# A gMLP and dilated-attention layer on one core: values re-laid in DRAM, projection weights in longer rows, and a warm-up bank of its own

## The chip, the core and the metric

The kernel runs on one core of a Trainium2 chip. The core has a matrix engine (TensorE, PE in the profile, with its weight loads shown apart as PEld), a vector engine (VectorE, DVE), a scalar engine (ScalarE, ACT), a general engine (GpSimd, POOL) and a sync engine (SyncE, SP) that here only issues DMA transfers. Each engine works through its own list of instructions in order; semaphores make an instruction wait for one on another engine or for a transfer. The metric is the device time of one execution in microseconds. It is the median of several executions, and the profile is that of one of them.

## The reference

One layer, sequence 1024, model width 1024, all in float32. Cut to what matters:

```python
h = rms_norm(x, g_pre)
u_a, v_a, z_a, q_b, k_b, v_b, z_b, gate_a, gate_b = split(h @ w_in)   # widths 3 x 2048, then 6 x 1024
y_a = spatial_gating(gelu(u_a), gelu(v_a), ln_g, ln_b, w_s, b_s) * silu(z_a)
# spatial_gating: u * (W_s LayerNorm(v) + b), W_s mixing 128 positions for each of 16 channel groups
y_b = mixture_of_dilations(q_b, k_b, v_b) * silu(z_b)
# 8 heads of 128; windows (128, dilation 1), (512, 4), (2048, 16), each +-64 keys, ALiBi,
# the three outputs weighted by their softmax denominators
m = sigmoid(gate_a + b) * (y_a @ w_pa) + sigmoid(gate_b + b) * (y_b @ w_pb)
out = x + rms_norm(m @ w_o, g_post)
```

## The kernel before

Every float32 operand of a matmul is split into a high and a low part (`hi`, `lo`), and a product is three matmuls: hi·hi, hi·lo, lo·hi. For a weight, `operand()` (L104 to L109) does the split: ACT copies the raw tile to `wh_...` (L106), then POOL, or DVE in a few places, subtracts to get `wl_...` (L108). Raw weight tiles `wr_...` come from DRAM through `raw_tile()` (L111 to L114), always on the SP queue, into three buffers, or into two buffers of another pool for the second half of a block.

The program has these stages.

1. **Start** (to about 60 us). Eight tiles of x are loaded, normalised (`norm_tile`, L244) and transposed on PE into the matrices `hT00`, `hT01`, `hT10`, `hT11`, together with sums of quarters of h (`t1` to `t4`). Warm-up matmuls on a tile of zeros (`warm`, L227) run ahead, around the product that spreads the gain vector over 128 partitions (`gpre`, L231 to L235). The bank with the tag "tp" that the warm-up writes is also the bank that the squares of `norm_tile` (`sqx`, L253) write.
2. **Values of the attention** (`vb`, to about 150 us), eight products of 128 rows each in two column halves. Their split halves go to DRAM, `v_hi` and `v_lo`, 1024 rows of 1024 each.
3. **Values of the gMLP** (`va0` to `va3`, about 161 to 322 us). Each group is one Strassen-like block of seven products, `p1, p6, p2, p7, p5, p4, p3` (`STEPS`, L377). A product of a group is 48 matmuls. Product `p1` needs the first half of the raw weights alone (tiles `wr_va100` and `wr_va101` for group 1: group, half j, quarter q), product `p6` needs `s2 = w10 + w11 - w00`, which DVE computes (L391) from the first half and the second half (`wr_va110`, `wr_va111`). The results pass gelu on ACT (`v_use`, L523), DVE takes statistics (L525), and SP stores them to `v_d` (L527), eight stores a group.
4. **Loop over g = 0, 2, ..., 14** (about 322 to 1020 us). Each iteration computes `u` and `z` for two channel groups, then one to two further blocks (`q`, `k`, `zb` for two heads, or gates), and between their products the spatial mixing of the normalised `vn`, read back from `v_d`. The blocks are the same seven products of 12 matmuls each (`features`, L443). Block u0 reads `wr_u00` for `p1` and `wr_u00` with `wr_u01` for `p6`.
5. **Attention** (about 1020 to 1330 us), eight heads, with the product of the gMLP branch, `y_a @ w_pa`, put between their pieces (`mlp_products`, L911 to L916). Its weights come from `mlp_weights` (L883), 32 loads of 512 KB, each a tile of eight 128-row blocks by 128 columns, held for two operands. The attention values of a head come by `residue_values` (L636) and `chunk_values` (L644): the chunk values lie row by row of one residue modulo 4, so that a head takes 4 residues x 2 halves x 2 pieces (`va`, the inner seven chunks, and `ve`, both ends) = 16 transfers.
6. **Tail** (to the end): the product with `w_pb`, the gates, `w_o`, the closing norm.

The Python text issues work in the order above, but the order in which an engine meets its instructions is set by the framework's list scheduler: it takes ready instructions by its own costs and priorities, so that a load stands in the SP queue where the scheduler put it, not where the text has it. `tc.issue_after(x)` tells it to put an instruction behind x. A store on the SP queue waits there until its data are computed, and what stands behind it on that queue waits with it.

## Time and profile before

| | |
|---|---|
| time, median of three runs | 1565.2 us (1562.21 to 1565.73) |
| the profiled execution's own time | 1563.55 us |
| its span in the profile | 1561.8 us, 22765 instructions |
| PE busy | 1511.7 us (97%) |
| PE weight loads | 1275.1 us (82%) |
| DVE, POOL, ACT busy | 872.5, 780.5, 683.0 us |
| DMA traffic | 251.64 MB, mean 161 GB/s |
| granted PE clock, mean | 0.99 |

The profile's page lists busy time of each engine, the span in 40 slices, the DMA queues, the chain of work that ended last, the costliest groups of instructions and the DMA issues with their time to landing. The trace behind it can be asked for stretches of time: what each engine did, what an instruction waited for, and the granted clock. A row of the timeline gives the start, the duration, the engine, the line of the kernel, the operation, output and inputs by name, a count, and in brackets the idle time ahead of it with the engine whose work ended it. Engine names with a q (SPq) are the issues of a DMA on that engine's queue. Tile names there are cut short: `va0u` is any tile of group va0 whose name begins so.

### The profile page before, as it was taken

To read this page: it belongs to the slowest core of one execution; us is meant where nothing else is said; L and a number is where in the kernel's file an instruction comes from. 1 tells how busy PE (TensorE), PEld (TensorE's weight loads), DVE (VectorE), ACT (ScalarE), POOL (GpSimd) and SP (SyncE) were. 2 spreads that over 40 slices of the span, in tenths; PEclk is the share of its full clock that TensorE was granted. 3 is DMA by queue.
4 is the path that set the end of the run, shared out by engine and by line. 5 is a ranking of instruction groups with operands and counts; after the bars stand their busy time and mean duration, and the time that the engine had idled before them with its cause. 6 is when DMAs were issued, how large, how long until landed. Compare 5 with 4: busy or idle time off the path is not lost.

```text
span 1561.8 us, 22765 instructions
## 1 busy us (share of the span) xinstructions
PE 1511.7 (97%) x7865; PEld 1275.1 (82%) x7865; DVE 872.5 (56%) x1699; ACT 683.0 (44%) x1318; POOL 780.5 (50%) x711
## 2 busy tenths in 40 slices
PE   8999999999999999999999999998999889999998
PEld 4787999988888888788888888877887778878886
DVE  5622544476665675766665565567877768232112
ACT  5522433343443433343445454577666755431111
POOL 2322644465565555555555555536555545473132
PEclk9999999999999999999999999999999999999999
DMA  6445533343434453544534353388687765885531
GB/s 230 162 135 190 161 109 102 113 130 123 153 121 148 126 171 115 152 138 138 165 108 156 101 176 109 123 244 255 201 226 199 225 209 179 250 270 166 187 108 68
DMA packets 247798, 251.64 MB, mean 161 GB/s; under 512 B 14297, under 2 KB 187385, under 8 KB 247426
## 3 DMA queue, kind: packets, MB, share of 16 engines
q1 hardware_dynamic: 247456, 249.88, 51.1%
q8 instruction: 62, 1.02, 0.3%
q14 instruction: 54, 0.44, 0.1%
q10 hardware_dynamic: 226, 0.30, 0.1%
HBM read 173.58 MB, written 76.55 MB: 160 GB/s over the span
## 4 chain that ended last, share of the span: by engine, by line
PE 71%; DVE 9%; issue 7%; ACT 4%; POOL 4%; DMA 4%; SPq 0%; ACTq 0%; POOLq 0%; DVEq 0%
PE pb L1040 2%; PE pb L1041 2%; PE pb L1039 2%; PE vb L154 2%; PE vb L156 2%; PE vb L155 2%; PE sg L560 2%; PE pa L916 2%; PE pa L914 2%; PE pa L915 2%; ACT st L704 1%; POOL out L1060 1%; PE pr L791 1%; DMA vn<-v_d 1%; DVE st L752 1%
## 5 line engine op out<-in xcount | busy, mean ns | idle before, releaser
L108 POOL TENSOR_TENSOR wl_pa<-wr_pa,wh_pa 128x512 fp32r<-128x512 f32 x56 | 74.6, 1342 | 42.3 <-ACT wh_pa L106 32.7
L704 ACT ACTIVATE st<-st,own 128x256 f32<-128x256 f32 (+1 forms) x128 | 62.6, 493 | 36.1 <-DVE own L700 36.1
L549 DVE TENSOR_SCALAR vn<-vn,mean,rstd 128x128 f32<-128x128 f32 x128 | 56.6, 497 | 36.4 <-DMA vn<-v_d 36.0
L1039 PE MATMUL pb<-yh,wh_pb 128*128 128x512 f32 x128 | 49.9, 390 | 2.0 <-ACT yh L159 2.0
L106 ACT ACTIVATE wh_pa<-wr_pa 128x512 fp32r<-128x512 f32 x64 | 38.7, 623 | 28.1 <-DMA wr_pa<-in_w_proj_a_dram 19.6
L1040 PE MATMUL pb<-yl,wh_pb 128*128 128x512 f32 x128 | 50.0, 391 | 0.4 <-DVE yl L159 0.2
L1041 PE MATMUL pb<-yh,wl_pb 128*128 128x512 f32 x128 | 49.8, 389 | 0.0
L717 DVE COPY oth<-own 32x4 f32<-32x4 f32 x128 | 36.2, 283 | 14.8 <-ACT st L704 13.3
L1074 ACT ACTIVATE sq<-o 128x512 f32<-128x512 f32 x16 | 9.6, 598 | 74.6 <-PE o L1072 74.6
L159 POOL TENSOR_TENSOR vl<-vn,vh 128x512 fp32r<-128x512 f32 x32 | 41.3, 1292 | 0.8 <-ACT vh L159 0.8
L1043 POOL TENSOR_TENSOR mb<-thb,mb 128x512 f32<-128x512 f32 x16 | 20.6, 1287 | 41.7 <-DVE thb L1042 28.1
L159 POOL TENSOR_TENSOR qcl<-q,qch 128x512 fp32r<-128x512 f32 x16 | 27.1, 1699 | 28.6 <-ACT qch L159 28.6
L717 POOL COPY oth<-own 32x4 f32<-32x4 f32 x128 | 24.0, 188 | 30.9 <-ACT st L704 26.2
L1054 DVE TENSOR_TENSOR sso<-sso 128x1 f32<-128x1 f32 x8 | 1.3, 160 | 67.6 <-ACT sq L1074 67.6
L752 DVE TENSOR_SCALAR st<-st,nm 128x256 f32<-128x256 f32 x64 | 38.1, 637 | 0.3
L164 POOL TENSOR_TENSOR sso<-sso,mhalf 128x1 f32<-128x1 f32 x8 | 4.4, 550 | 59.1 <-DVE sso L163 59.1
L159 DVE TENSOR_TENSOR ptlb<-pb,pthb 128x512 fp32r<-128x512 f32 x32 | 22.0, 687 | 20.5 <-ACT pthb L159 20.5
L859 POOL TENSOR_TENSOR o<-o,zt 128x512 f32<-128x512 f32 x16 | 20.6, 1291 | 25.7 <-DMA zt<-z_d 13.7
L108 POOL TENSOR_TENSOR wl_wos<-wr_wos,wh_wos 128x512 fp32r<-128x512 f32 x16 | 20.7, 1291 | 22.8 <-ACT wh_wos L106 22.8
L700 DVE CUSTOM_DVE_ANT_0 st<-sc,tb 128x256 f32<-128x256 f32 x64 | 23.5, 416 | 14.0 <-PE sc L697 12.6
L1039 PEld LDWEIGHTS pb<-yh,wh_pb 128*128 128x128 f32 x128 | 24.0, 188 | 7.4 <-ACT yh L159 2.4
L772 PE MATMUL pb<-ident,st 128*128 128x128 f32 x128 | 21.0, 286 | 8.3 <-DVE st L752 5.5
(2648 smaller groups left out, 5842.0 us busy)
## 6 DMA issues: line engine op xcount, KB each, us to landing
wr_pa<-in_w_proj_a_dram SPq DMA_DIRECT2D x32, 512.0 KB, 5.8
wr_g<-in_w_in_dram SPq DMA_DIRECT2D x16, 512.0 KB, 3.6
wr_va<-in_w_in_dram SPq DMA_DIRECT2D x16, 512.0 KB, 3.7
wr_u<-in_w_in_dram SPq DMA_DIRECT2D x16, 512.0 KB, 4.0
wr_z<-in_w_in_dram SPq DMA_DIRECT2D x16, 512.0 KB, 4.0
vn<-v_d SPq DMA_DIRECT2D x32, 256.0 KB, 3.1
y_d<-s SPq DMA_DIRECT2D x32, 256.0 KB, 2.4
wr_yf<-y_d SPq DMA_DIRECT2D x16, 512.0 KB, 5.0
```

The costliest lines, as they stand in the source:

```text
L106: nc.scalar.activation(hi, src, AF.Copy)
L108: low.tensor_tensor(lo, src, f32(hi), ALU.subtract)
L154: nc.tensor.matmul(ps, lhs[k][0], rh, start=(k == 0), stop=False)
L155: nc.tensor.matmul(ps, lhs[k][0], rl, start=False, stop=False)
L159: return nc.scalar.activation(hi, src, AF.Copy), low.tensor_tensor(lo, src, f32(hi), ALU.subtract)
L549: nc.vector.tensor_scalar(vn[:, c, :], vn[:, c, :], mean[:, 4 * b + c, 0:1], rstd[:, 4 * b + c:4 * b + c + 1], op0=ALU.subtract, op1=ALU.mult)
L704: nc.scalar.activation(st[:, t, :n], st[:, t, :n], AF.Exp, bias=own[:, half, idx, 0:1], scale=-1.0, accum_out=own[:, half, idx, 1:2])
L717: (nc.gpsimd, nc.vector)[half].tensor_copy(dst, src)
L752: nc.vector.tensor_scalar(w, w, f, None, op0=ALU.mult)
L1039: nc.tensor.matmul(ps, lh, rh, start=(k == 0), stop=False)
L1040: nc.tensor.matmul(ps, lh, rl, start=False, stop=False)
L1041: nc.tensor.matmul(ps, ll, rh, start=False, stop=(k == KT - 1))
```

## The change

Three edits.

- **The warm-up bank.** The warm-up matmuls write a bank with the tag "sc" in place of "tp", and there is one more of them ahead of the `gpre` product. The two ACT copies that take the spread gain out of its bank move behind the squares of the first tile.
- **Attention values in the chunks' row order.** New DRAM tensors `va_d` (7 x 4 x 32 rows of 1024, high and low) and `ve_d` (2 x 4 x 16 rows of 1024, high and low) hold copies of the rows of `v_hi` and `v_lo`, sorted by chunk and residue. `value_rows()` makes them with 24 transfers from DRAM to DRAM on the SP queue: 8 of 7 x 32 x 1024 floats (917 KB each) and 16 of 16 x 1024 floats (64 KB each). The text takes one of its eight steps at the head of each iteration of the g loop. `chunk_values` then reads a head's values with four transfers. The bytes that a head reads stay the same, and so does the length of a contiguous piece (128 floats).
- **Projection weights.** `mlp_weights` loads tiles of four 128-row blocks by 256 columns, so that a contiguous piece is 1 KB in place of 512 bytes. The number of loads (32) and their size (512 KB) stay. Two raw tiles now feed four operands together (before, one fed two), and the second of the four already needs the second tile; the buffers for raw tiles stay three.

```diff
@@ -176,6 +176,9 @@
         return [dram.tile(shape, F32, name=f"{name}_{s}") for s in "hl"]
 
     v_hi, v_lo = hi_lo("vb", [S, DB])
+
+    va_d = hi_lo("va", [7, 4, 32, DB])
+    ve_d = hi_lo("ve", [2, 4, 16, DB])
     o_d = dram.tile([H, P, S], F32, name="o_d")
     t4_d = hi_lo("t4", [P, 4, 512])
     q_d = dram.tile([H, P, S], F32, name="q_d")
@@ -222,16 +225,16 @@
         nc.scalar.activation(first[:, P:P + 1], mhalf, AF.Square)
         idle = wpool.tile([P, 512], BF16, tag="th", bufs=2, name="idle")
         nc.vector.memset(idle, 0.0)
-        pt = bank("tp", "warm")
+        pt = bank("sc", "warm")
 
         def warm(n):
             for _ in range(n):
                 nc.tensor.matmul(pt, idle[:, :P], idle, start=True, stop=True)
 
-        warm(4)
-        for j, pg in enumerate(banks("mm mm", "gpre")):
+        warm(5)
+        spread = banks("mm mm", "gpre")
+        for j, pg in enumerate(spread):
             nc.tensor.matmul(pg, ones, grow[:, 512 * j:512 * (j + 1)], start=True, stop=True)
-            nc.scalar.activation(gpre[:, 512 * j:512 * (j + 1)], pg, AF.Copy)
         warm(8)
 
         def transposed(hl, i, src, name):
@@ -242,7 +245,7 @@
             split(*[t[:, :, i * P:(i + 1) * P] for t in hl], pt.rearrange("p (k n) -> p k n", k=4))
             return last
 
-        def norm_tile(c, load=1):
+        def norm_tile(c, load=1, between=None):
             b, i = divmod(c, 4)
             for _ in range(load):
                 load_tile()
@@ -251,6 +254,8 @@
             sq = bank("tp", f"sqx{c}")
             for j in range(2):
                 squared = nc.scalar.activation(sq, xt[:, 512 * j:512 * (j + 1)], AF.Square, accum_out=ss[:, j:j + 1])
+            if between:
+                between(squared)
             nc.vector.tensor_tensor(ss[:, 0:1], ss[:, 0:1], ss[:, 1:2], ALU.add)
             power(ss[:, 1:2], ss[:, 0:1], 1.0 / D)
             for j in range(2):
@@ -318,7 +323,12 @@
             nc.scalar.activation(wb, pb, AF.Copy)
             nc.sync.dma_start(wsb_d[q].rearrange("p g n -> p (g n)"), wb)
 
-        squared, turned = norm_tile(0, 0)
+        def norm_weights(squared):
+            for j, pg in enumerate(spread):
+                with tc.issue_after(squared.ins):
+                    nc.scalar.activation(gpre[:, 512 * j:512 * (j + 1)], pg, AF.Copy)
+
+        squared, turned = norm_tile(0, 0, norm_weights)
         rows = sp.tile([32, P], F32, name="rows")
         wv = []
         for k in range(0, KT, 2):
@@ -579,8 +589,19 @@
             lambda h=h: features(w_in, OFF_K + h * P, f"k{h}", store_parts(k_d[h:h + 2])),
             lambda h=h: features(w_in, OFF_ZB + h * P, f"zb{h}", gate_z(h)))]
         others += [lambda m=m: gates(m) for m in range(2, 16, 2)]
+        def value_rows():
+
+            for vd, va_, ve_ in zip((v_hi, v_lo), va_d, ve_d):
+                for r in range(4):
+                    nc.sync.dma_start(va_[:, r], vd[64:960].rearrange("(a i r) n -> r a i n", i=32, r=4)[r])
+                    for c in range(2):
+                        nc.sync.dma_start(ve_[c, r], vd[960 * c:960 * c + 64].rearrange("(i r) n -> r i n", r=4)[r])
+                    yield
+
+        rows_moved = value_rows()
         for g in range(0, G, 2):
             us, ts = {}, {}
+            take(rows_moved, 1)
 
             def u_use(i, b, _, c, src):
                 nc.scalar.activation(c, src, AF.Gelu_apprx_tanh)
@@ -645,14 +666,11 @@
 
             hs = slice(h * P, (h + 1) * P)
             res["va"], res["ve"] = [], []
-            for s, vd in enumerate((v_hi, v_lo)):
+            for s in range(2):
                 a_ = ap.tile([P, 7, E], F32R, tag=f"va{s}", name=f"va{s}{h}")
                 e_ = ap.tile([64, 2, E], F32R, tag=f"ve{s}", name=f"ve{s}{h}")
-                va_src = vd[64:960, hs].rearrange("(a i r) e -> r i a e", i=32, r=4)
-                ve_src = vd.rearrange("(c i r) n -> r i c n", i=16, r=4)
-                for r in range(4):
-                    nc.sync.dma_start(f32(a_[32 * r:32 * (r + 1)]), va_src[r])
-                    nc.sync.dma_start(f32(e_[16 * r:16 * (r + 1)]), ve_src[r][:, 0:16:15, hs])
+                nc.sync.dma_start(f32(a_), va_d[s].rearrange("a r i n -> (r i) a n")[:, :, hs])
+                nc.sync.dma_start(f32(e_), ve_d[s].rearrange("c r i n -> (r i) c n")[:, :, hs])
                 res["va"].append(a_)
                 res["ve"].append(e_)
 
@@ -881,11 +899,11 @@
 
         def mlp_weights():
             for b, p, half in MLP_ORDER:
-                for m in (2 * p, 2 * p + 1):
-                    raw = raw_tile(w_pa[8 * half * P:8 * (half + 1) * P, m * P:(m + 1) * P].rearrange(
-                        "(k p) n -> p k n", p=P), f"pa{b}{m}{half}")
+                raw = [raw_tile(w_pa[4 * q * P:4 * (q + 1) * P, 2 * p * P:2 * (p + 1) * P].rearrange(
+                    "(k p) n -> p k n", p=P), f"pa{b}{p}{q}") for q in (2 * half, 2 * half + 1)]
+                for m in range(2):
                     for g in range(2):
-                        yield operand(raw[:, 4 * g:4 * g + 4, :], f"pa{b}{m}{half}{g}",
+                        yield operand(raw[g][:, :, m * P:(m + 1) * P], f"pa{b}{2 * p + m}{half}{g}",
                                       nc.vector if (b, p) == (0, 0) else nc.gpsimd)
 
         def mlp_products(ya):
```

The scheduler answers with another order in several places. On the SP queue, from the end of block g0 (stores to `th_d`) through group va0, the order before is (`wr_va110`: second half j = 1, quarter 0 of the weights of group va1; `v_d<-va0...`: stores of the results of va0):

```order
L509 DMA th_d_92<-g0u20_1236 128x512
L113 DMA wr_va110_1847<-in_w_in_dram 128x2x512
L113 DMA wr_va111_1851<-in_w_in_dram 128x2x512
L527 DMA v_d_93<-va0c000_1563 128x2x256
L527 DMA v_d_93<-va0c001_1568 128x2x256
L113 DMA wr_va201_2325<-in_w_in_dram 128x2x512
L113 DMA wr_va300_2797<-in_w_in_dram 128x2x512
L527 DMA v_d_93<-va0u30_1635 128x2x256
L527 DMA v_d_93<-va0u31_1637 128x2x256
L527 DMA v_d_93<-va0c100_1763 128x2x256
L527 DMA v_d_93<-va0c101_1769 128x2x256
L527 DMA v_d_93<-va0u20_1435 128x2x256
```

On SP at the same place with the change (`va_h<-vb_h`: the first of the new copies):

```order
L519 DMA th_d_96<-g0u20_1241 128x512
L596 DMA va_h_86<-vb_h_84 7x32x1024
L537 DMA v_d_97<-va0c000_1568 128x2x256
L537 DMA v_d_97<-va0c001_1573 128x2x256
L537 DMA v_d_97<-va0u30_1640 128x2x256
L537 DMA v_d_97<-va0u31_1642 128x2x256
L537 DMA v_d_97<-va0c100_1768 128x2x256
L537 DMA v_d_97<-va0c101_1774 128x2x256
L537 DMA v_d_97<-va0u20_1440 128x2x256
L537 DMA v_d_97<-va0u21_1442 128x2x256
L113 DMA wr_va110_1852<-in_w_in_dram 128x2x512
L113 DMA wr_va111_1856<-in_w_in_dram 128x2x512
```

The loads `wr_va110` and `wr_va111`, which stood ahead of all stores of group va0, now stand behind the last of them, `va0u21`. The same happens to the second halves of va2 and va3. At the end of va3, before, with the second half for block u0:

```order
L543 DMA vn01_3765<-v_d_93 128x4x128
L113 DMA wr_u01_3303<-in_w_in_dram 128x4x256
L113 DMA wr_z01_3445<-in_w_in_dram 128x4x256
L527 DMA v_d_93<-va3c000_2991 128x2x256
L527 DMA v_d_93<-va3c001_2996 128x2x256
L113 DMA wr_q00_3611<-in_w_in_dram 128x4x256
L527 DMA v_d_93<-va3u30_3063 128x2x256
L527 DMA v_d_93<-va3u31_3065 128x2x256
L527 DMA v_d_93<-va3c100_3191 128x2x256
```

On SP at the same place with the change:

```order
L537 DMA v_d_97<-va3c100_3196 128x2x256
L537 DMA v_d_97<-va3c101_3202 128x2x256
L537 DMA v_d_97<-va3u20_2868 128x2x256
L537 DMA v_d_97<-va3u21_2870 128x2x256
L113 DMA wr_u01_3311<-in_w_in_dram 128x4x256
L113 DMA wr_z01_3453<-in_w_in_dram 128x4x256
L553 DMA vn00_3664<-v_d_97 128x4x128
```

`wr_u01` and `wr_z01` stood ahead of the stores of va3 and now stand behind the last. Block k0's second half, `wr_k01`, likewise moved behind `q_d<-q0u20`, the last store of q0.

On ACT, the operand copies follow the loads. Before, from the last operand of p1 of va1 (the `wh_va1p6...` are the operands of p6; `va0...<-va0...` at L523 the gelus of the group before):

```order
L106 ACTIVATE wh_va1p11_1883<-wr_va101_1849 128x512
L106 ACTIVATE wh_va1p60_1921<-ws_va10s2_1919 128x512
L523 ACTIVATE va0u30_1635<-va0u30_1635 128x512
L106 ACTIVATE wh_va1p61_1953<-ws_va11s2_1951 128x512
L523 ACTIVATE va0u31_1637<-va0u31_1637 128x512
L106 ACTIVATE wh_va1p20_1983<-wr_va110_1847 128x512
L523 ACTIVATE va0c100_1763<-va0c100_1763 128x512
L106 ACTIVATE wh_va1p21_2011<-wr_va111_1851 128x512
L523 ACTIVATE va0c101_1769<-va0c101_1769 128x512
L106 ACTIVATE wh_va1p70_2053<-ws_va10s3_2051 128x512
L523 ACTIVATE va0u20_1435<-va0u20_1435 128x512
```

On ACT at the same place with the change:

```order
L106 ACTIVATE wh_va1p11_1888<-wr_va101_1854 128x512
L533 ACTIVATE va0u30_1640<-va0u30_1640 128x512
L533 ACTIVATE va0u31_1642<-va0u31_1642 128x512
L533 ACTIVATE va0c100_1768<-va0c100_1768 128x512
L533 ACTIVATE va0c101_1774<-va0c101_1774 128x512
L533 ACTIVATE va0u20_1440<-va0u20_1440 128x512
L533 ACTIVATE va0u21_1442<-va0u21_1442 128x512
L416 ACTIVATE va1u20_1916<-va1p10_1858 128x512
L416 ACTIVATE va1u21_1918<-va1p11_1859 128x512
L106 ACTIVATE wh_va1p60_1926<-ws_va10s2_1924 128x512
L106 ACTIVATE wh_va1p61_1958<-ws_va11s2_1956 128x512
```

The operands of p6 of va1 stood between the gelus of va0; they now stand behind all of them and behind the two copies of va1's own p1 result (`va1u20`, `va1u21`). The order of the products on PE is the same there.

At the start of the program, on ACT before (`sqx0` the squares of the first tile, `gpre` the spread gain, `wh_vb0...` the first value weights):

```order
L222 ACTIVATE first_124<-mhalf_76 128x1
L234 ACTIVATE gpre_122<-gpre_0_134 128x512
L234 ACTIVATE gpre_122<-gpre_1_135 128x512
L253 ACTIVATE sqx0_151,ss0_150<-xt0_120 128x512 x2
L106 ACTIVATE wh_vb0_0_176<-wr_vb0_0_174 128x512
L106 ACTIVATE wh_vb0_1_180<-wr_vb0_0_174 128x512
```

On ACT at the start with the change:

```order
L225 ACTIVATE first_128<-mhalf_76 128x1
L256 ACTIVATE sqx0_154,ss0_153<-xt0_124 128x512 x2
L329 ACTIVATE gpre_126<-gpre_0_139 128x512
L106 ACTIVATE wh_vb0_0_181<-wr_vb0_0_179 128x512
L329 ACTIVATE gpre_126<-gpre_1_140 128x512
L106 ACTIVATE wh_vb0_1_185<-wr_vb0_0_179 128x512
L256 ACTIVATE sqx4_192,ss4_191<-xt4_189 128x512
```

The squares (`sqx`) of the first tile moved ahead of the copies of `gpre`.

## The prediction

> **What bounds the kernel now.** I read the page first, then a table of stages, then the start, the group values and the attention in the timeline.
>
> ```profile
> span 1561.8 us, 22765 instructions
> PE 1511.7 (97%) x7865; PEld 1275.1 (82%) x7865; DVE 872.5 (56%) x1699; ACT 683.0 (44%) x1318; POOL 780.5 (50%) x711
> ...
> PE 71%; DVE 9%; issue 7%; ACT 4%; POOL 4%; DMA 4%; SPq 0%; ACTq 0%; POOLq 0%; DVEq 0%
> ```
>
> PE is busy for all but 50.1 us (1561.8 - 1511.7). The change adds one warm-up matmul to PE and removes none of its products, so it can only move those 50 us, the stretches at a lower granted clock, or make new idle time. The profiled execution took 1563.55 us, 1.75 us more than its span and 1.65 us less than the median of 1565.2; my sum is made against 1563.55. The columns of the table of stages are the stretch, its length, busy us (instructions) of PE, PEld, DVE, ACT and POOL, the granted PE clock, the DMA share and GB/s:
>
> ```profile
> 0.00:18.00 18.00, 11.62 (x26) 4.63 (x27) 6.52 (x14) 7.13 (x15) 4.14 (x9) 1.00 0.61 219
> 160.00:320.00 160.00, 160.00 (x1329) 159.69 (x1328) 81.43 (x141) 63.22 (x104) 81.99 (x62) 1.00 0.36 115
> 320.00:400.00 80.00, 79.45 (x370) 65.91 (x368) 54.31 (x100) 30.89 (x52) 49.03 (x42) 1.00 0.42 133
> 1010.00:1060.00 50.00, 42.69 (x213) 34.27 (x211) 34.03 (x92) 33.02 (x70) 22.77 (x30) 0.98 0.79 237
> 1060.00:1330.00 270.00, 254.16 (x1526) 217.21 (x1526) 202.85 (x565) 178.19 (x445) 150.14 (x210) 0.97 0.72 212
> ```
>
> The reader should see two things. There is something to win at the start (6.4 us idle in 18) and in attention (7.3 and 15.8 us idle, the last at a clock of 0.97). In the gMLP values (160 to 320 us) there is nothing to win: PE is busy for 160.00 of 160 us. Any wait that arises there is a loss in full.
>
> **The start, the warm-up bank: a gain of 4.0 us.**
>
> ```profile
> 10.55 0.60 ACT L253 ACTIVATE sqx<-xt 128x512 f32<-128x512 f32 x1 [2.08 <-PE warm L229]
> ...
> 7.77 2.74 PE L229 MATMUL warm<-idle 128*128 128x512 bf16 x6
> 14.94 1.11 PE L241 MATMUL xT<-ident,xt 128*128 128x128 f32 x4 [4.43 <-DVE xt L258]
> 17.38 0.78 PE L154 MATMUL vb<-wh_vb,hT00h 128*128 128x512 f32 x1
> ```
>
> The squares wait for the warm-up, whose bank they share, and PE's transposes then wait for them: 14.94 - 10.55 = 4.4 us from squares to transpose. With another bank the squares need only the x tile and can run where ACT now idles, ahead of 10.55 by several us. The transposes are then held by PE's own queue: the warm-up ended at 7.77 + 2.74 = 10.51 and has one matmul more (2.74 / 6 = 0.46), so they begin at about 11.0, 3.9 to 4.0 us earlier. The first product at 17.38 follows by the same distance. Bounds: -6 (the loads that wait for a buffer start earlier too) and -1.5 (the clock reaches full speed later against the work, or weights arrive late). I take -4.0, the difference of the rows.
>
> **The value copies: new waits in the gMLP values, a loss of 23.5 us.** The copies have few instructions: 24 issues on SP, which has idle time. But the order that comes with them moves the second weight halves behind the last store of the group before. The rows of the present trace for the seam between va0 and va1:
>
> ```profile
> 175.38 1.62 SPq L113 DMA_DIRECT2D wr_va<-in_w_in_dram  x2
> 202.45 1.40 SPq L527 DMA_DIRECT2D v_d<-va0u  x2
> ...
> 201.05 0.28 PE L469 MATMUL va1p<-wh_va1p,hT00h 128*128 128x256 f32 x1
> 206.81 0.28 PE L469 MATMUL va1p<-wh_va1p,t2h 128*128 128x256 f32 x1
> ...
> 204.35 0.69 DVE L391 TENSOR_TENSOR ws_va11s<-wr_va,ws_va11s 128x512 f32<-128x512 f32 x1 [1.14 <-POOL wl_va1p L108]
> 204.19 0.63 ACT L106 ACTIVATE wh_va1p<-ws_va10s 128x512 fp32r<-128x512 f32 x1 [0.73 <-PE va1p L472]
> 204.90 1.29 POOL L108 TENSOR_TENSOR wl_va1p<-ws_va10s,wh_va1p 128x512 fp32r<-128x512 f32 x1 [0.59 <-ACT wh_va1p L106]
> ...
> wr_va<-in_w_in_dram SPq DMA_DIRECT2D x16, 512.0 KB, 3.7
> wr_u<-in_w_in_dram SPq DMA_DIRECT2D x16, 512.0 KB, 4.0
> ```
>
> Now the load is issued at 175.38 and p6 begins at 206.81, 31 us later. With the change it stands behind the two stores that end at 202.45 + 1.40 = 203.85. From there: landing 3.7 (207.55), DVE makes s1 and s2, 2 x 0.69 (208.93), ACT copies 0.63 (209.56), POOL subtracts 1.29 (210.85). PE has p1 alone to cover it, from 201.05 to 206.81, and its second matmul of p6 needs the low part at 206.9: a stall of 4.0 us. Three seams (va1, va2, va3) give 12.0 us. On ACT nothing else helps or hurts: the gelus that now stand ahead are due before the weights land.
>
> Blocks u0 and k0 have a shorter cover:
>
> ```profile
> 322.01 0.40 PE L444 MATMUL u0p<-hT00h,wh_u0p 128*128 128x512 f32 x1
> 325.12 0.47 PE L444 MATMUL u0p<-t2h,wh_u0p 128*128 128x512 f32 x1 [0.20 <-ACT va3u L523]
> 382.22 0.40 PE L444 MATMUL k0p<-hT00h,wh_k0p 128*128 128x512 f32 x1
> 384.96 0.39 PE L444 MATMUL k0p<-t2h,wh_k0p 128*128 128x512 f32 x1
> 382.18 0.32 SPq L480 DMA_DIRECT2D q_d<-q0u  x1
> ```
>
> For u0 the same chain counts from 322.01: stores done 2.8 later (203.85 - 201.05), landing 4.0, then 1.38 + 0.63 + 1.29: 322.01 + 10.1 = 332.1 against 325.12, a stall of 7.0 us. For k0 the store is issued at 382.18, the load at 382.5, and 382.5 + 4.0 + 3.3 = 389.8 against 384.96, less about 0.5 us of mixing matmuls that now stand between p1 and p6 (two pairs at 381.74 to 382.22 in the present order): 4.5 us. The sum is 12.0 + 7.0 + 4.5 = 23.5 us. Bounds: each of the five between 1 us less (a load lands in 2.7) and 1.5 us more (it shares the queues with stores just issued), 18 to 31.
>
> **The clock after such stalls: a loss of 7 us.** What a stall of this length does shows at the head of attention:
>
> ```profile
> 1058.63 0.47 PE L772 MATMUL pb<-ident,st 128*128 128x128 f32 x1 [4.90 <-DVE st L752]
> ...
> 1058.60:1063.50 4.90, 4.17 (x15) 3.10 (x15) 4.16 (x7) 3.45 (x7) 3.27 (x4) 0.50 0.56 192
> 1065.00:1070.00 5.00, 5.00 (x26) 4.11 (x25) 2.89 (x3) 2.38 (x4) 5.00 (x4) 1.00 0.85 274
> ```
>
> After 4.90 us of idling PE ran 4.9 us at half clock, which costs up to 2.45 us of work. Five stalls at 0 to 2.45 are 0 to 12 us; I take 1.4 each, 7 us, since PE also waited within that stretch. [...]
>
> The copies' own traffic I set at nothing: 8.4 MB read and written beside 251.6 MB, at a DMA share of 0.36 to 0.42, and no load that PE needs soon stands right behind a large copy. If that cover is gone, it is the second rival.
>
> **Attention: a gain of 6 us.** The longest wait there, chain rows in order of time, and the DMA rows:
>
> ```profile
> 1042.17 5.97 DMA wr_pa<-in_w_proj_a_dram
> 1048.22 1.15 ACT wh_pa L106 x2
> ...
> 1042.60 1.25 SPq L654 DMA_DIRECT2D va<-vb_h  x1
> 1052.10 0.44 SPq L655 DMA_DIRECT2D ve<-vb_l  x1
> ...
> wr_pa<-in_w_proj_a_dram SPq DMA_DIRECT2D x32, 512.0 KB, 5.8
> ```
>
> A projection load of 512-byte pieces takes 5.8 us, one of the same size in 1 KB pieces (`wr_u`) 4.0. The 4.90 us wait hangs on such a load: 1.8 us less of landing, by a chain that goes on through ACT and DVE, and the clock stretch after it shortens. The 16 value issues hold SP from 1042.60 to 1052.54, 10 us, ahead of the next loads; four leave 2.5. But most of the other idle pieces are 0.3 to 2.6 us behind DVE (for instance 3.0 us in seven waits of score products on it), which the change does not touch, and the first projection product now has one tile's weights less ready, since the second tile is behind the first. So: -2 to -4 for the long wait, -2 to -4 for shorter waits of operands, 0 for DVE. The stage's whole idle time with its clock loss, 23.1 + 8, bounds the gain; a reordered prologue that leaves PE without filler in head 0's four score pairs bounds the loss at +6. I take -6.
>
> **Sum.** 1563.55 - 4.0 + 23.5 + 7 - 6 = 1584.05, so 1584.
>
> **Rivals.**
>
> *The waits do not arise, or are small (faster).* If the loads behind the last store land before p6 is due, then the change is start and attention alone: 1563.55 - 4.0 - 6 = 1553.5, and with the attention's whole share up to 1540. It turns faster when the five stalls with their clock sum to less than 10 us, 2 us each. For it: PE would need cover of 10 us where a group's p1 is 5.76. The order against it is fixed, and the landing would have to fall from 3.7 to 1.7.
>
> *The copies crowd the queues (slower still).* A copy of 917 KB ahead of normalised-value or weight loads delays them. Loads of `vn` already end 36.0 us of DVE's idling:
>
> ```profile
> L549 DVE TENSOR_SCALAR vn<-vn,mean,rstd 128x128 f32<-128x128 f32 x128 | 56.6, 497 | 36.4 <-DMA vn<-v_d 36.0
> q1 hardware_dynamic: 247456, 249.88, 51.1%
> ```
>
> 249.88 MB in 51.1% of 16 engines x 1561.8 us is 19.6 KB per engine and us, so a copy takes 917 / (16 x 19.6) = 2.9 us if it spreads over all 16, and 6.7 over seven. Eight copies that each delay PE by 2 us beyond its cover add 16: 1600. Against it: PE waited little in this stage and SP's stores, not loads, follow the copies. [...]
>
> *Attention gains enough to cancel.* If the 1 KB rows and the free SP queue take away 20 of the 31 us, the result is 1584 - 14 = 1570, still slower.
>
> **Chances.** Measurements of this kernel can tell about 0.2%, 3 us. The forecast and its near variants (all five stalls, 1575 to 1597): 0.61. Crowded queues above 1597: 0.10. Attention or smaller stalls between 1566 and 1575: 0.12. No waits, faster: 0.12; gains and losses that cancel within 0.2%: 0.05. The range of 8 in 10 is 1565 to 1598. Faster 0.12, same 0.05, slower 0.83.
>
> **What would show it.** The transposes of the first tile start at about 11 us; `sqx` waits for no warm-up. PE shows idle pieces of 4 us before p6 of va1, va2 and va3, of 7 before p6 of u0 and 4.5 before p6 of k0, each released by POOL's `wl` of that operand, with `wr_va11` issued just after the last `v_d` store; the busy time of 160 to 340 us falls from full. The granted clock drops after several of them. `wr_pa` lands in about 4 us and the wait at the head of attention is shorter than 4.9. I am wrong if p6 starts without a gap, which would mean that the loads are issued earlier than the order says or that something else covers them, or if attention gives back more than 15 us.

## The result and the profile after

The changed kernel takes 1645.97 us (median of 4 runs, 1643.12 to 1647.25) against 1565.47 us for the kernel before: ratio 1.0514, 95% interval 1.0494 to 1.0534. The loss is 80.5 us where the prediction said about 20. Head and chain of waits on PE in the profile of the changed kernel (engine, tile, line, who ended the wait: us in total, times, longest):

```profile
span 1645.1 us, 22691 instructions
PE 1536.0 (93%) x7866; PEld 1294.4 (79%) x7866; DVE 895.2 (54%) x1699; ACT 681.4 (41%) x1318; POOL 785.0 (48%) x711
...
PE u4p L454 <- DVE u4u L425: 8.5, 1, 8.5
PE pa L790 <- DVE ptle L159: 7.1, 2, 4.8
PE u0p L454 <- ACT wh_u0p L106: 6.8, 1, 6.8
PE u0p L454 <- DVE u0u L425: 6.7, 1, 6.7
PE zb2p L454 <- ACT wh_zb2p L106: 6.6, 1, 6.6
PE zb2p L454 <- DVE zb2u L425: 5.6, 1, 5.6
PE k0p L454 <- ACT wh_k0p L106: 4.9, 1, 4.9
PE va1p L479 <- ACT wh_va1p L106: 4.1, 1, 4.1
PE va2p L479 <- ACT wh_va2p L106: 4.1, 1, 4.1
PE va3p L479 <- ACT wh_va3p L106: 4.0, 1, 4.0
```

PE's idle time rose from 50.1 to 109.1 us (1645.1 - 1536.0), and its busy time from 1511.7 to 1536.0 although its products are the same: that part is matmuls at a lower granted clock (0.963 on average over the span, 0.990 before; in p6 of va1 single matmuls took up to 0.58 us, in its other products 0.28). Six of the ten waits in this list are for ACT's operand copies (`wh_...`) of product p6; five of these were forecast, that of `zb2` was not. Three are for DVE's additions (`...u`) in u4, u0 and zb2, which no term of the prediction had. The one of `pa` belongs to attention.

Where in the program the time goes is seen from the first matmul of each stage. All lengths are in us, worked out from the start of the stage's first matmul in each trace (the tail is up to the first matmul of the closing product; what follows it is 95.5 in both).

| kernel | to va0 | values va0 to va3 | g = 0 to 6 | g = 8 to 14 | attention | tail |
|---|---|---|---|---|---|---|
| before | 154.2 | 167.8 | 345.1 | 360.8 | 348.0 | 90.4 |
| changed | 147.5 | 189.8 | 416.3 | 361.4 | 343.0 | 91.5 |
| difference | -6.7 | +22.0 | +71.2 | +0.6 | -5.0 | +1.1 |

The start gained 6.7 us and attention 5.0, near the forecast of 4.0 and 6. The values and the first half of the loop lost 93 us. The scheduler took the copies out of the places that the text gives them: four of the eight large ones were issued during the values (from 159.70 us on) and four in the loop. The first and the last of those in the loop, from SP's timeline:

```profile
360.58 0.78 SPq L596 DMA_DIRECT2D va_l<-vb_l  x1
...
561.60 0.78 SPq L596 DMA_DIRECT2D va_l<-vb_l  x1
```

Two stretches of the changed kernel, busy time by engine, clock and DMA share as in the prediction's table:

```profile
160.00:340.00 180.00, 164.92 (x1300) 162.85 (x1298) 77.68 (x143) 54.27 (x91) 72.57 (x57) 0.94 0.32 104
340.00:765.00 425.00, 370.92 (x1597) 302.31 (x1596) 259.91 (x380) 140.94 (x233) 215.71 (x158) 0.93 0.42 133
```

In the values PE is no longer busy throughout, and the DMA share is lower (0.32, it was 0.36), not higher. The clock is 0.94 there and 0.93 in the loop. From g = 8 on (753.6 us), behind the last of the copies (640.62), the loop runs as before.

The seam between va0 and va1 in the changed kernel, from the timelines of SP, DVE, ACT and PE:

```profile
195.57 0.36 SPq L537 DMA_DIRECT2D v_d<-va0u  x1
196.03 0.95 SPq L113 DMA_DIRECT2D wr_va<-in_w_in_dram  x2
...
201.26 0.69 DVE L401 TENSOR_TENSOR ws_va10s<-wr_va,wr_va 128x512 f32<-128x512 f32 x1 [4.93 <-DMA wr_va<-in_w_in_dram]
202.77 0.63 ACT L106 ACTIVATE wh_va1p<-ws_va10s 128x512 fp32r<-128x512 f32 x1 [2.83 <-DVE ws_va10s L401]
203.46 0.80 PE L479 MATMUL va1p<-wh_va1p,t2h 128*128 128x256 f32 x2 [4.15 <-ACT wh_va1p L106]
205.19 0.58 PE L481 MATMUL va1p<-wl_va1p,t2h 128*128 128x256 f32 x1 [0.93 <-POOL wl_va1p L108]
...
203.50:210.20 6.70, 5.77 (x27) 5.47 (x28) 0.57 (x2) 3.83 (x8) 6.70 (x6) 0.54 0.69 222
```

The chain has the steps of the prediction: last store, load, sums, copy, low part. The sums could start 5.2 us after the issue of the load (196.03 to 201.26), where the prediction counted 3.7. PE waited twice, 4.15 us for ACT's copy and 0.93 us for POOL's low part. The last row is the stretch after the stall: a mean granted clock of 0.54 over 6.70 us.

### The profile page after: what moved, and what is told of

Read it like the earlier page. It is cut to its first block, busy times and chain, and to the rows that moved or that the text cites. A ratio compares the mean times of both kernels' runs of the same rounds, so it can differ in the third digit from the quotient of the medians.

```text
span 1645.1 us, 22691 instructions
## 1 busy us (share of the span) xinstructions
PE 1536.0 (93%) x7866; PEld 1294.4 (79%) x7866; DVE 895.2 (54%) x1699; ACT 681.4 (41%) x1318; POOL 785.0 (48%) x711
## 4 chain that ended last, share of the span: by engine, by line
PE 43%; DMA 5%; issue 4%; DVE 4%; POOL 3%; ACT 2%; SPq 0%; POOLq 0%; DVEq 0%; ACTq 0%
PE pa L932 2%; PE pa L934 2%; PE pa L933 2%; PE pb L1058 2%; PE pb L1059 2%; PE pb L1057 2%; DMA krl<-k_d 2%; PE pr L809 1%; POOL out L1078 1%; PE sg L570 1%; PE pc L824 1%; DMA wr_yf<-y_d 1%; DVE oth L735 1%; PE sc L714 1%; DMA vn<-v_d 1%
## 5 line engine op out<-in xcount | busy, mean ns | idle before, releaser
L559 DVE TENSOR_SCALAR vn<-vn,mean,rstd 128x128 f32<-128x128 f32 x128 | 66.5, 575 | 24.2 <-DMA vn<-v_d 24.2
L159 POOL TENSOR_TENSOR vl<-vn,vh 128x512 fp32r<-128x512 f32 x32 | 42.5, 1328 | 42.0 <-ACT vh L159 42.0
L770 DVE TENSOR_SCALAR st<-st,nm 128x256 f32<-128x256 f32 x64 | 42.1, 701 | 0.3
L574 DVE SCALAR_TENSOR_TENSOR s<-sg,lng,wsb 128x256 f32<-128x256 f32 x64 | 27.9, 475 | 14.2 <-PE sg L570 14.2
L159 ACT ACTIVATE vh<-vn 128x512 fp32r<-128x512 f32 x32 | 20.2, 631 | 23.0 <-PE sg L570 20.2
```

The source lines that it names most:

```text
L159: return nc.scalar.activation(hi, src, AF.Copy), low.tensor_tensor(lo, src, f32(hi), ALU.subtract)
L559: nc.vector.tensor_scalar(vn[:, c, :], vn[:, c, :], mean[:, 4 * b + c, 0:1], rstd[:, 4 * b + c:4 * b + c + 1], op0=ALU.subtract, op1=ALU.mult)
L770: nc.vector.tensor_scalar(w, w, f, None, op0=ALU.mult)
```

## The experiments

Two theories are held against each other. **Order**: the loss comes from where the scheduler now puts weight loads and, through them, the work on DVE. **Traffic**: it comes from the copies' 8.4 MB in the DMA queues. Either can hold for a part of the loss.

### Each edit by itself

Warm-up bank alone (the first and last of the diff's parts on the start):

```diff
-        pt = bank("tp", "warm")
+        pt = bank("sc", "warm")
...
+        squared, turned = norm_tile(0, 0, norm_weights)
```

> The kernel before with the warm-up bank edit alone. In the changed kernel the first product began 6.3 us earlier and the blocks at 156 us 7.7 us earlier than before, ahead of any copy. My theory: this edit alone gives that, 6 to 8 us, about 1558 us. Rival: part of the lead is eaten by waits later on (attention, the tail are bound by others), then 1560 to 1564.

Measured: 1558.9 us against 1565.61, ratio 0.9963 (0.995 to 0.9976). The theory's range came, and the whole 6.7 us stays to the end.

Projection weights alone:

```diff
-                for m in (2 * p, 2 * p + 1):
-                    raw = raw_tile(w_pa[8 * half * P:8 * (half + 1) * P, m * P:(m + 1) * P]...
+                raw = [raw_tile(w_pa[4 * q * P:4 * (q + 1) * P, 2 * p * P:2 * (p + 1) * P]...
+                    for q in (2 * half, 2 * half + 1)]
```

> The kernel before with the projection weights in rows of 1 KB alone, chunk values in sixteen transfers. In the changed kernel these loads land in 4.2 us (5.8 before) and the delay against the kernel before shrank by about 4 to 8 us over the attention. My theory: this edit gives most of that, 3 to 8 us, 1557 to 1562. Rival: the gain in attention belongs to the four transfers, then this edit is within 3 us of 1565, or slower, since two raw tiles are now needed at once.

Measured: 1581.28 us, ratio 1.0107 (1.0088 to 1.0126), a loss of 15.7 us where the theory expected a gain; the rival allowed for a loss. Attention took 363.2 us in place of 348.0. The waits of SP's queue in attention, before and then with long rows alone:

```profile
SPq L113 <- POOL wl_pa L108: 15.3, 4, 6.1
```

```profile
SPq L113 <- POOL wl_pa L108: 41.5, 15, 11.3
```

SP waits 41.5 us in 15 places, not 15.3 in 4, for POOL to be done with a raw tile before it can issue the next load. All other loads of attention stand behind that wait. Two raw tiles are held for four operands and there are three buffers.

Copies and four transfers alone (the parts of the diff on `va_d`, `ve_d`, `value_rows`, `chunk_values`):

```diff
+            take(rows_moved, 1)
...
+                nc.sync.dma_start(f32(a_), va_d[s].rearrange("a r i n -> (r i) a n")[:, :, hs])
```

> The kernel before with the copies and the four transfers alone. Both theories, order (the place in which the scheduler now puts loads and vector work) and traffic (the copies' own bytes in the DMA queues), put the whole loss here: 1645.97 + 7 (no start gain) + about 4, 1650 to 1660. If it is under 1620, the three edits harm each other instead.

Measured: 1646.44 us in one run, 3.6 us under the expected range. The loss is all here: values 189.9, g = 0 to 6 415.0 us. Attention took 339.4, 8.6 less than before: the four transfers are a gain by themselves, and with the long rows besides attention took 343.0, 3.6 more.

### The copies ahead of the values

```diff
+        take(rows_moved)
         with tc.tile_pool(name="values", bufs=1) as vp:
...
-            take(rows_moved, 1)
```

> The changed kernel with all eight copy steps issued ahead of the gMLP values in the text, on the same queue. The second weight halves then stand ahead of the last stores again, as in the kernel before; the bytes copied are the same, though they move within one stretch ahead of group va0 and its neighbours. Theory order: the stalls before p6 of va1, va2, va3, u0, k0 vanish and so do the waits on the vector engine after them: start and attention gains remain, 1550 to 1560, plus up to 10 us if the copies hold up the weights of va0. Theory traffic: the same 8.4 MB cost the same wherever they run, 1620 to 1650.

Measured: 1601.85 us, ratio 1.024 (1.0219 to 1.0262). Neither number came. Values took 214.2 us, of which 43.8 are one wait, and the loop is as before (346.1 and 360.7). The stretch of that wait (busy time of the five engines, then granted clock, DMA share, GB/s):

```profile
165.00:203.00 38.00, 0.00 (x0) 0.00 (x0) 1.52 (x3) 0.00 (x0) 0.00 (x0) 0.50 0.60 220
```

Seven large copies stand here ahead of the weights of va0, and PE waits for them once, for 44 us. Behind that none of the stalls of the changed kernel is left.

The same with the large copies written 32 x 7 x 1024 rather than 7 x 32 x 1024:

```diff
-                    nc.sync.dma_start(va_[:, r], vd[64:960].rearrange("(a i r) n -> r a i n", i=32, r=4)[r])
+                    nc.sync.dma_start(va_[:, r].rearrange("a i n -> i a n"),
+                                      vd[64:960].rearrange("(a i r) n -> r i a n", i=32, r=4)[r])
```

> The run with all copies ahead of the gMLP values waited 43.8 us for the weights of va0, behind seven large copies of about 6.2 us each. Here each large copy is written with its slowest dimension 32 rather than 7, the same bytes and rows of 4 KB. [...] Theory seven engines: a copy takes 6.2 x 7 / 16 = 2.7 us, the wait falls to 15 to 22 us, the total to 1572 to 1582. Rival: the copies are bound by memory, not by the count of engines; then the wait stays at 40 us and the total at 1600.

Measured: 1584.81 us in one run; the wait fell to 29.75 us, between the two forecasts. The stretch of the wait here, and then the part in which the copies alone ran, here and in the run before:

```profile
162.00:187.00 25.00, 0.00 (x0) 0.00 (x0) 1.09 (x2) 0.00 (x0) 0.00 (x0) 0.50 0.99 338
...
162.00:174.00 12.00, 0.00 (x0) 0.00 (x0) 0.00 (x0) 0.00 (x0) 0.00 (x0) 0.50 1.01 347
...
168.00:186.00 18.00, 0.00 (x0) 0.00 (x0) 0.00 (x0) 0.00 (x0) 0.00 (x0) 0.50 0.50 192
```

With slowest dimension 32 the DMA share was 1.01, at 347 GB/s; with 7 it was 0.50, at 192 GB/s. So the first shape left half of the DMA engines' time unused. That is near the 7 of 16 (0.44) of the theory of seven engines, but on how many engines a copy ran no run shows. The wait fell by a third and not by more, since it is not made of copies alone: the forecast had scaled the whole of it. From the first large copy of this block to the issue of the first load of va0 behind the copies it is 25.3 us before (161.27 to 186.60) and 14.5 here (159.76 to 174.26); from there until PE goes on it is 17.2 us (203.79) and 14.0 (188.25), and that part holds the loads and their operands.

### Order alone, without a copy

```diff
+        if pool and name[:3] in ("va1", "va2", "va3", "u01", "z01", "k01"):
+            with tc.issue_after(behind["q" if name[0] == "k" else "v"].ins):
+                return raw_load(src, name, pool)
```

`behind` holds the last store of the block before.

> The kernel before without any copy: the second weight halves of va1, va2, va3, u0, z0 and k0 are ordered to be issued behind the last store of the block before (issue_after), as they stand in the changed kernel. Theory order: idle pieces of 4 to 5 us before p6 of va1, va2, va3, 7 of u0, 4 to 5 of k0, each with 2 to 3 us of half clock behind it, 1565 + 35 to 45 = 1600 to 1610; more if the vector engine's waits in u0 and k0 also come (up to 1620). Rival traffic: without copies no such idle pieces, within 5 us of 1565.

Measured: 1620.99 us in one run, 57 us over the kernel before, with not one byte copied. PE's longest waits in it on the moved blocks, from its list of waits:

```profile
PE u0p L452 <- ACT wh_u0p L106: 7.7, 1, 7.7
...
PE k0p L452 <- DVE k0u L423: 6.9, 1, 6.9
...
PE va3p L477 <- ACT wh_va3p L106: 3.9, 1, 3.9
PE u0p L452 <- DVE u0u L423: 3.8, 1, 3.8
...
PE va1p L477 <- ACT wh_va1p L106: 3.4, 1, 3.4
```

The number is just over the upper end (1620), since DVE's waits in u0 and k0 came too; the wait before p6 of k0 was only 0.9 us. Values took 189.5 us (changed kernel 189.8), g = 0 to 6 375.5 (416.3). The displaced loads of the values make the whole loss of that stage; those of u0, z0 and k0 make 30 of the 71 us of the loop. Order alone, without copies, is thus 52 of the 93 us. Here the changed kernel's other moved transfers keep their old places, and there are no copies: the 41 us left are not told apart by this run. Two of those other moves show in the changed kernel's SP queue, each with the store that it stands behind:

```profile
522.40 0.32 SPq L511 DMA_DIRECT2D z_d<-zb0u  x1
...
523.25 0.55 SPq L113 DMA_DIRECT2D wr_u<-in_w_in_dram  x1
...
615.16 0.46 SPq L502 DMA_DIRECT2D k_d<-hik_d  x1
615.67 0.55 SPq L113 DMA_DIRECT2D wr_zb<-in_w_in_dram  x1
```

They are the second halves for u4, issued 7.4 us ahead of that block's first matmul (45.4 us in the kernel before), and for zb2, issued 2.9 us behind it (42.5 us ahead before). PE's waits in u4 (8.5) and zb2 (6.6 and 5.6) come with them; in the run with the order alone, where both loads keep their places, there are none. That reads as order once more, but no run moves these two loads alone.

### The copies on another queue

```diff
-                    nc.sync.dma_start(va_[:, r], ...
+                    nc.scalar.dma_start(va_[:, r], ...
```

> The changed kernel with the 24 copies issued on the scalar engine's queue instead of SP's, one step at the head of each g iteration as in the change. On SP the second weight halves then stand ahead of the last stores, as before. Theory order: the 78 us that the values and the first g iterations lost (160 to 760 us of the changed kernel) shrink to under 8, since the same 8.4 MB now run with the weights in their old places; start gain 7, attention gain 5 as in the changed kernel: 1550 to 1565. Rival traffic: bytes in the same stretch of time cost the same, 1620 to 1650.

Measured: 1566.75 us, ratio 1.0027 (1.0015 to 1.0038). The weights are back in their places, the copies have the same shape and the same bytes as in the changed kernel, and g = 0 to 6 took 344.8 us: nothing of the loss of the loop is left. But here the scheduler issued all eight large copies from 138.38 to 280.71 us, ahead of the loop, so that this run does not say what a copy in the loop costs. The values, with the copies beside them, took 182.6 us, 14.8 more than before; 12.5 of it is one wait near 160 us, where a copy runs beside the weights of va0, and it puts the time just over the upper end. Beside that wait PE idled for 0.9 us in the values. With projection weights in short rows besides:

> As the run with the copies on the scalar engine's queue, but projection weights in rows of 512 bytes as before. Attention took 348.0 us before, 363.2 with the long rows alone, 339.4 with the four transfers alone and 343.0 with both. Theory: the long rows cost attention 3 to 4 us beside the four transfers, so this is 3 to 4 us faster than that run, 1547 to 1560. Rival: long rows only hurt by the order of their own run and make no difference here.

Measured: 1564.83 us, ratio 1.0014 (1.0001 to 1.0027), about 2 us less, and attention 337.8 us against 340.3. The intervals overlap, so the difference is not shown, and the time missed the expected range.

### The copies held back

```diff
+                    with tc.issue_after(held.ins):
+                        moves = [nc.scalar.dma_start(va_[:, r], ...)]
...
+                    held = moves[0]
```

The first copy is held behind the last gelu of va3, each other one behind the copy before.

> Warm-up bank and four transfers, projection rows as before, copies on the scalar engine's queue and each held behind the last gelu of the gMLP values and behind the copy before it. The run with copies on that queue had one long wait left, 12.5 us near 160 us behind a copy issued at 138 us beside the weights of va0, and some 7 us of half clock. Theory: without a copy there that wait goes, and the loads keep their places; 1565 - 7 (start) - 9 (attention, 339 to 348 us) = 1546 to 1553. Rival: the copies, now within the first g iterations, delay normalised values or weights there by 10 us or more: 1556 to 1565.

Measured: 1559.72 us, ratio 0.9964 (0.9952 to 0.9977). The values are clean (166.8), but g = 0 to 6, in which all eight large copies now run (319.90 to 437.69 us), took 353.2 us, 8.1 more than before, with one wait of 4.3 us in u0. The rival's range came: the gain of the four transfers was lost again there. In that wait DVE stood idle for a load of normalised values, issued at 334.56 beside a copy issued at 331.90:

```profile
342.79 1.11 DVE L561 TENSOR_SCALAR vn<-vn,mean,rstd 128x128 f32<-128x128 f32 x4 [10.66 <-DMA vn<-v_d]
```

Held only behind va1:

> As the run with held copies, but held only behind the gelus of group va1, so that the first four copies run beside the weight loads of va2 and va3, as in the changed kernel, on another queue. Theory order: no wait before p6 of va2 or va3, within 3 us of the run with held copies. Rival traffic: waits of 2 us or more there.

Measured: 1572.35 us in one run, 12.6 over the run with held copies: a wait of 1.6 us before p6 of va3, and 361.6 us for g = 0 to 6. Neither theory's figure came; since the loads of va3 keep their places, the wait there is not one of order. One copy behind each iteration's gelus of u:

> As the run with held copies, but each of the eight steps is held behind the gelus of u in its own iteration of the g loop, so that the copies are spread over 340 to 1000 us. The held run kept the start and attention gains (7 and 8 us) and lost 8 us in the first g iterations, most of it one wait of 4.3 us in block u0, where the chained copies stood on the scalar engine's queue. Theory: spread out they cost nothing, 1548 to 1554. Rival: each copy costs about 1 us wherever it stands in the loop, 1556 to 1560.

Measured: 1591.08 us, ratio 1.0173 (1.0155 to 1.0191), the largest miss of these. In each iteration PE waits 3.2 to 4.3 us in z; g = 0 to 6 took 362.0 us and g = 8 to 14 took 385.7, 16.9 and 24.9 more than before. The rows of the timelines of POOL and DVE at g = 4, where the copy was issued at 508.40, and the landing time of the stores `wo_l` (a weight of the tail, split and put aside in the loop) here, and then that landing time in the kernel before:

```profile
516.61 1.29 POOL L108 TENSOR_TENSOR wl_k2p<-wr_k,wh_k2p 128x512 fp32r<-128x512 f32 x1 [3.70 <-DMA wo_l<-wl_wos]
519.18 1.77 DVE L401 TENSOR_TENSOR ws_zb2s<-wr_zb,wr_zb 128x512 f32<-128x512 f32 x1 [5.33 <-POOL wl_k2p L108]
525.08 1.74 DVE L401 TENSOR_TENSOR ws_zb2s<-ws_zb2s,wr_zb 128x512 f32<-128x512 f32 x1 [1.18 <-POOL wl_k2p L108]
527.34 0.68 DVE L425 TENSOR_TENSOR z4u<-z4p,z4u 128x512 f32<-128x512 f32 x1
...
wo_l<-wl_wos SPq DMA_DIRECT2D x16, 256.0 KB, 6.9
```

```profile
wo_l<-wl_wos SPq DMA_DIRECT2D x16, 256.0 KB, 2.1
```

Here the copies' traffic does cost: the stores `wo_l` land in 6.9 us rather than 2.1 (medians), POOL waits 3.70 us for its buffer, DVE waits 5.33 us for POOL, and the addition that PE needs stands behind on DVE. So traffic did cost here, where a copy ran beside a transfer that something needed, and the four copies in the loop of the changed kernel can have cost something too: loads of `vn` landed in 4.7 us there (median), 3.1 before.

### Long rows, one tile at a time

```diff
-                for m in (2 * p, 2 * p + 1):
-                    for q in (2 * half, 2 * half + 1):
+                for q in (2 * half, 2 * half + 1):
+                    for m in (2 * p, 2 * p + 1):
```

> The kernel before with the projection weights in rows of 1 KB, but the two operands of one tile are used next to each other (the product runs over the quarter first, then over the two output blocks), so that a raw tile is given back after two operands, as before the change. Long rows alone cost 15.7 us, with SP's queue waiting 41.5 us in attention for POOL's lower parts to free a raw tile, 15.3 before. Theory (two tiles held in three buffers): SP's wait falls below 25 us and the time to 1560 to 1570. Rival (the longer rows or their loads themselves are at fault): 1575 to 1585 again.

Measured: 1576.59 us, ratio 1.0077 (1.005 to 1.0104). SP's wait for POOL fell to 27.0 us in 7, attention to 358.5 us. The rival's range came. Holding two tiles explains about 5 of the 15.7 us at most, and since the intervals of the two runs overlap not even that is clear; the rest stays open.

> The held copies, the warm-up bank, the four transfers, and long rows with one tile at a time: everything that the change does, in an order that costs no wait that I know of. Theory: 1540 to 1552, as the run with held copies or a few us less, from loads that land in 4 us rather than 5.8. Rival: long rows bring nothing, within 3 us of the run with held copies, or the reordered product costs: 1552 to 1560.

Measured: 1561.44 us, ratio 0.9989 (0.9977 to 1.0001), attention 339.9 us, as the run with held copies (339.8). The rival came: long rows bring nothing beside the four transfers.

### The change's own queue and place, another order

The one difference from the changed kernel is that the large copies are written 32 x 7 x 1024, with the same diff as above. The scheduler then gives SP another order at the seam between va0 and va1, and the last large copy comes at 290.01:

```profile
156.24 0.34 SPq L519 DMA_DIRECT2D th_d<-g0u  x1
156.63 0.57 SPq L596 DMA_DIRECT2D va_h<-vb_h  x1
165.03 0.37 SPq L113 DMA_DIRECT2D wr_va<-in_w_in_dram  x1
167.71 1.30 SPq L537 DMA_DIRECT2D v_d<-va0c  x2
...
290.01 0.57 SPq L596 DMA_DIRECT2D va_l<-vb_l  x1
```

The load for va1 stands ahead of va0's stores again, and all eight large copies now run during the values (145.0 to 311.8 us); none is left in the loop.

> The changed kernel with one difference: each large copy is written with slowest dimension 32 instead of 7, on SP's queue and in the same place of the text. The scheduler then leaves the second weight halves of all groups ahead of the last store (first copy, then the load for va1). Theory order: the waits before p6 of va1 to va3, u0, k0 go, and the time falls from 1646 to 1555 to 1580 (copies of some 4 us, one of them right ahead of the weights of va1; the long rows stay in). Rival (bytes of the copies in the queues): nothing but the share by the faster copies comes back, 1610 to 1640.

Measured: **1551.73 us, ratio 0.9919 (0.9896 to 0.9942)**, 94 us less than the changed kernel and faster than the kernel before. That is just under the expected range. Stages: 145.0, 166.8, 344.9, 361.1, 340.8, 91.5. The head of its profile and its values:

```profile
span 1545.7 us, 22707 instructions
PE 1506.9 (97%) x7866; PEld 1276.6 (83%) x7866; DVE 866.2 (56%) x1699; ACT 684.9 (44%) x1318; POOL 777.1 (50%) x711
...
145.00:312.00 167.00, 167.00 (x1370) 165.94 (x1369) 84.26 (x152) 65.40 (x107) 83.71 (x67) 1.00 0.54 169
```

The same 8.4 MB are read and written, at a DMA share of 0.54 in the values where the changed kernel had 0.32, and PE is busy for 167.00 of 167 us. In the values eight copies on this queue, in this shape, thus cost PE nothing, where four stood in the changed kernel: its 22.0 us there are no price of the bytes. That the 71 us of the loop are gone as well does not tell order from traffic, since the loads are back in their places and the copies have left the loop, both at once. Shape, order and time of the copies changed together in this run.

> As the run before, with projection weights in rows of 512 bytes. Attention alone is changed: 339 to 340 us in place of 341 to 343. Theory: 0 to 4 us less than that run. Rival: the two runs differ by more than 5 us, then the rows of the weights matter through the order of attention.

Measured: 1553.72 us, ratio 0.9927 (0.9905 to 0.9949). The two differ by 2 us within their intervals, so neither expectation is shown. In the profiles attention was 337.6, 3.2 less, but the loop 5.6 and the start 4.9 more: at the start a filling of `shift` on DVE, ahead of the first normalisation, waits 2.55 us until the warm-up matmuls have let go of its buffer (normalisation at 11.45, it was 8.60 in the changed kernel).

## Why the prediction was wrong

The direction was right, and so was the mechanism as far as it went: late second halves that stall p6. The size was not: +80.5 us against a range that ended at +34. The step that failed is the sum's "a loss of 23.5 us", which counts the five stalls as all that the new order does, together with the 7 us for the clock. The runs showed 71.2 us of loss in g = 0 to 6 alone, 50.2 of it idle time and 21.0 lost clock, where the prediction had two stalls of 11.5 us together and some 3 us of clock.

- **Start, -4.0**: measured -6.7, shown by the warm-up edit alone. The transposes began at 9.63, not at 11: the second warm-up was done at 8.02, with matmuls of 0.24 us where the prediction counted 0.46, and PE then waited 1.61 us for DVE's normalisation. PE's own warm-up was not the bound that the prediction took it for.
- **Five stalls, +23.5**: measured 4.15, 4.10, 4.03 for va1 to va3 (4.0 forecast), 6.8 for u0 (7.0), 4.9 for k0 (4.5), 24.0 in all. These pieces were ended by ACT's copy and not by POOL's `wl`, as the prediction had it; behind all but u0's PE waited another 0.9 us for POOL. With them it is 27.7 us, within the forecast's 18 to 31. That the first pieces come so near the forecast is luck: 4.0 was counted up to the low part, for which it was 5.0 to 5.1, and the landing was 5.2, not 3.7. The order alone reproduces four of the five.
- **The clock, +7**: under-sized. The values lost 22.0 us with 14.3 us more idle time, so 7.7 for three stalls, 2.6 each where I took 1.4. The loop's clock took 21 more (71.2 - 50.2), where the prediction left some 3 of its 7. My one row of the kernel before was cut too short: the half clock goes on into the next row of the same table, which has 0.70 over 1.50 us, so that it lasted about 5.8 us and the bound was 2.9, not 2.45:

```profile
1063.50:1065.00 1.50, 1.48 (x5) 1.14 (x5) 1.50 (x2) 1.50 (x3) 1.50 (x2) 0.70 0.08 24
```

  The 0.54 over 6.70 us behind the first stall likewise makes about 6.2 us at half clock. The 1.4 was my estimate between nothing and 2.45; here none of the three stalls of 4 us went without: behind those of va2 and va3 the mean granted clock was 0.55 over 6.50 us (251.50 to 258.00) and 0.56 over 6.60 (299.40 to 306.00).
- **The term that was not there** is the main miss. In g = 0 to 6 PE's idle time rose by 50.2 us. The p6 waits of u0 and k0 are 11.8 of these. One more late second half (`zb2`, 6.6) the prediction did not have, and the rest, about 32, are for the most part waits of p4 and others for DVE. How such a wait arises, from DVE's timeline in block u0 of the changed kernel, with the matmul that waits:

```profile
357.19 1.79 DVE L401 TENSOR_TENSOR ws_z0s<-wr_z,ws_z0s 128x512 f32<-128x512 f32 x1
358.90 5.00 DVE L559 TENSOR_SCALAR vn<-vn,mean,rstd 128x128 f32<-128x128 f32 x4
363.83 0.68 DVE L425 TENSOR_TENSOR u0u<-u0p,u0u 128x512 f32<-128x512 f32 x1
...
367.14 0.68 DVE L425 TENSOR_TENSOR u0u<-u0p,u0u 128x512 f32<-128x512 f32 x1
367.96 0.76 PE L454 MATMUL u0p<-t401h,wh_u0p 128*128 128x512 f32 x1 [6.67 <-DVE u0u L425]
```

The loads of z0 and the normalised values stood ahead of the last stores before, so that DVE had their sums and normalisations done when u0 began. Now they land in u0 and DVE does them there, in front of the additions that free PE's banks. Four normalisations take 5.00 us, 1.25 each, where the mean in the kernel before was 0.497 us, and a sum takes 1.79 us here and 0.68 elsewhere; POOL is busy throughout this stretch. The whole trace of the changed kernel says the same: the 115 sums that ran with POOL idle took 0.67 to 0.70 us, the 31 that ran with POOL busy throughout 1.63 on average; the normalisations took 0.34 us (78 of them) and 1.23 (20); the additions that read a PSUM bank took 0.68 in both cases. No run changes POOL's work alone, so that the cause is read and not tested. Why the sums of two SBUF tiles and the normalisations, which read one tile, take longer then and the additions from PSUM do not, no run shows. The prediction asked what stands behind the late load on PE, ACT and POOL, but not what the late load puts on DVE's queue, and for whom that is late.
- **Attention, -6**: measured -5.0 in the change. But its parts were assigned wrongly: the four transfers give 8.6 (one run), and the long rows, which I had counted as a gain by their landing, cost 15.7 alone and 0 to 4 beside the four transfers. Their loads landed in 4.2 us in the changed kernel, as forecast, but in 5.5 with the long rows alone, against 5.8 before: the length of the pieces alone did not set it.
- **The rivals**: crowded queues were given 0.10 and the time above 1597. That is where the time lies, but for 52 of the 93 us it is not by that mechanism: without a byte copied they are lost as well. The prediction's own "copies' traffic at nothing" stands for the values, where eight copies on SP's queue, written 32 x 7 x 1024, left PE no idle time. For the loop it is not shown: with all second halves issued well ahead of their products, copies there cost 8.1 us (all eight on ACT's queue) and 16.9 us (four, one in each iteration). How much of the other 41 us is owed to them, and how much to the late loads of u4 and zb2, is open. One figure of the first rival is off as well: with the attention's whole share of 31 us its time is about 1528, not 1540. The seven engines in the second rival's 6.7 us, and in the forecast for the copies with slowest dimension 32, were an assumption that no run shows; what the runs showed while copies alone ran is a DMA share of 0.50 at 192 GB/s with slowest dimension 7 and of 1.01 at 347 GB/s with 32. What the shape decided was above all the order that the scheduler made around the copy. Why it puts the loads there no run shows.

## What to carry to other kernels

When an edit adds transfers and a scheduler orders the program, compare the new order on every queue before the transfers' bytes: a load that moves behind a store delays the sums, the operands and the work on each engine between them, and each of these has a queue of its own in which something else is late next. Ask also when the scheduler will run the transfers, since it need not be where the text has them. Price a stall together with the clock after it, here 2.6 us for a stall of 4 to 5. A copy's written shape can decide both its speed (192 or 347 GB/s here) and the order: try it before giving up the idea, since here the same bytes in another order of dimensions turned 5.1% slower into 0.8% faster.

## What the runs showed that was not expected

- A stall of 4.15 us was followed by 6.70 us at a mean granted clock of 0.54; the wait of 4.90 us in the kernel before by 4.90 us at 0.50 and 1.50 us at 0.70. Both make about 6 us at half clock.
- A sum of two SBUF tiles on DVE took 0.67 to 0.70 us with POOL idle and 1.63 on average with POOL busy throughout; an addition that reads a PSUM bank took 0.68 in both cases.
- While copies of 917 KB within DRAM ran, the DMA engines moved 192 GB/s at a share of 0.50 with slowest dimension 7, and 347 GB/s at 1.01 with 32.
- A store of 256 KB landed in 2.1 us in the kernel before (median) and in 6.9 us (median) in the run with one such copy an iteration on another queue.
- Projection loads in pieces of 1 KB made attention longer by 15.2 us (363.2 against 348.0), of which the holding of two raw tiles explains about 5 at most.
